# Second step of the rotary turn and the two sums with the attention sink on GpSimd instead of VectorE, in a two-layer hybrid decoder

## The chip, the cores and the metric

The kernel runs on one core of one Trainium2 chip. The metric is the device time of one execution in microseconds (us): the median of several runs of the same program. One execution was also taken by the hardware profiler; what is read from a trace is of that one.

The engines go by the profile's names: PE (TensorE, matrix products and transposes), PEld (its weight loads), DVE (VectorE), ACT (ScalarE), POOL (GpSimd), SP (SyncE, which here issues the transfers). Each works through its own list of instructions in order, and waits where an operand comes from another engine.

## What is computed

Two decoder layers over 512 tokens of width 1024, all in fp32. Each layer projects its input once into the queries, keys and values of two groups of heads and of an indexer, runs the two attentions, projects back, adds and normalises, and ends with a gated feed-forward part. Cut to what the change touches:

```python
def rope(x, positions):                       # x: queries or keys, last axis d = 64 or 32
    cos, sin = jnp.cos(ang), jnp.sin(ang)     # ang = positions * inv_freq, d/2 angles
    x1, x2 = x[..., :half], x[..., half:]
    return jnp.concatenate([x1 * cos - x2 * sin, x2 * cos + x1 * sin], -1)

def swa_sink_attention(q, k, v, sinks):       # group "a": window of 128 keys, 8 heads, 2 key heads
    s = jnp.einsum('bnqhgd,bnkhd->bnhgqk', qb, kb_window) * (D ** -0.5)   # masked
    m = jnp.maximum(s.max(-1, keepdims=True), sink)
    pr = jnp.exp(s - m)
    denom = pr.sum(-1, keepdims=True) + jnp.exp(sink - m)
    return (pr / denom) @ v_window

def dsa_sparse_attention(...):                # group "b": 8 heads, 1 key head
    # indexer: relu(qi . ki) weighted and summed over 8 heads of 32; the 128 best keys of each query
    # attention over these keys, no sink

def hybrid_layer(...):
    qa, ka, va, qb, kb, vb, qi, ki, wi = split(x @ w_in)
    # rope on qa, ka, qb, kb, qi and on layer_norm(ki)
    x = layer_norm(alpha * x + concat(oa, ob) @ w_o)
    x = layer_norm(alpha * x + ffn(x) + ple)
```

## The kernel before

The 512 tokens are four tiles of 128, with the tokens of a tile on the 128 partitions. A product of two fp32 matrices is made of three matmuls in the format fp32r: high times high, high times low and low times high (L316 to L318). So each operand is split: ACT copies it to fp32r (the high part), and POOL or DVE subtracts that from the fp32 original (the low part). For the weights SP fetches a block into one of three buffers `wst`, ACT copies (L269), POOL subtracts (L270) into one of five buffers `wsp`; the down projection does the same at L247 and L248.

A rotary turn (`rope`) has four instructions per call. DVE multiplies the projection's result, still in PSUM, by a table that holds cosine and sine beside each other, into a temporary `t2k` in SBUF (L474). The second step adds the two products, one of them with its halves swapped, within `t2k` (L476). ACT copies the sum to its high part in a `slot` (L479), and POOL makes the low part (L480). Later `turn` or the functions `turns` transpose the slot on PE (L486), and ACT copies the result out of PSUM (L487). Each layer makes 32 such calls: 16 for the queries of the two attentions (256 sums per partition), 8 for the queries of the indexer (128) and, for the keys, 2 + 4 smaller ones (64 or 128).

The indexer multiplies turned queries and keys (PE, L617), ACT applies relu (L619), DVE sums over heads (L620). Its keys are first normalised on DVE (from L526 over L350, L542 and L353 to L360 to L543), then turned. A search on DVE finds the 128 best keys: 16 rounds of L631 and L632 for each of three tiles.

Attention goes by units of four heads and 128 queries. `scores` runs PE (L656) and, for each head, a DVE instruction that adds the mask and keeps the row's minimum (L659). In group a, L664 takes the sink into that minimum. ACT makes the exponentials with their row sums (L666). For the sink, L669 adds sink and minimum (4 values per partition), ACT takes its exponential (L670), and L671 adds that to the row sums. DVE takes the reciprocal (L672), and POOL spreads it over 256 columns (`rb`, L674). `values` transposes the exponentials (L700), copies them (L703, L708), multiplies by the values (L694), transposes `rb` (L717), copies it (ACT, L720), scales (DVE, L725) and splits (L732, L733).

What is issued when is decided twice. A class `Order` interleaves the streams of work by ratios written into the kernel, and puts the transposes off behind the turn by fixed amounts of PE work (`D_GI, D_K, D_Q` of L36, `order.later`). Then the Tile scheduler, with a timeline of its own for the costs, arranges the instructions of each engine, so a change of an instruction's engine also moves others.

Of the kernel before, what the change touches and what calls it, by code (L numbers as in the profile page):

```python
# [14 lines left out]
OP = mybir.AluOpType  # L15
# [72 lines left out]
def hybrid_kernel(ctx: ExitStack, tc: tile.TileContext, x, p, positions, ln_in_g, ln_in_b, w_in,  # L88
# [3 lines left out]
    PE, V, A, G, SP = nc.tensor, nc.vector, nc.scalar, nc.gpsimd, nc.sync  # L92
# [11 lines left out]
    def bank(tag, bufs, dt=F32):  # L104
        return psum.tile([128, 512], dt, name="bank", tag="bank", bufs=8)
# [7 lines left out]
    def t2k(dt=F32):  # L113
        return tmp.tile([128, 512], dt, name="t2k", tag="t2k")

    def sm(n, name):
        return small.tile([128, n], F32, name=name, tag=name)
# [347 lines left out]
    def rope(src, t, n, d, hi, lo, dup, each=False):  # L465

        h = d // 2  # L470
        tab = tab64 if d == 64 else tab32
        tab = tab[:, t:t + n] if each else tab[:, t, None].to_broadcast([128, n, 2, d])
        t12 = t2k()[:, :2 * n * d].rearrange("p (n c d) -> p n c d", n=n, c=2)
        V.tensor_tensor(t12, src[:, :, None].to_broadcast([128, n, 2, d]), tab, OP.mult)  # L474
        t1, t2 = t12[:, :, 0], t12[:, :, 1]
        V.tensor_tensor(t1.rearrange("p n (u i) -> p n u i", u=2), t1.rearrange("p n (u i) -> p n u i", u=2),  # L476
                        t2.rearrange("p n (u i) -> p n u i", u=2)[:, :, ::-1], OP.add)
        s = t1 if dup == 1 else t1[:, :, None, :].to_broadcast([128, n, dup, d])
        A.copy(hi, s)  # L479
        G.tensor_tensor(lo, s, hi, OP.subtract)  # L480
# [30 lines left out]
    for l in range(L):  # L511
# [6 lines left out]
        def gi_out(t, ps):  # L518
# [10 lines left out]
            if t > 0:  # L529
                wi[t] = small.tile([128, IH], F32, name="wi", tag="wi", bufs=4)  # L530
                V.tensor_scalar(wi[t], ps[:, 288:296], IH ** -0.5 * ID ** -0.5, None, op0=OP.mult)
                qs = [slot(), slot()]
                r1 = ps[:, :256].rearrange("p (n d) -> p n d", n=IH)
                for j in range(2):
                    qv = qs[j].rearrange("p (n u s d) -> p n u s d", n=4, u=2, s=2)
                    rope(r1[:, 4 * j:4 * j + 4], t, 4, ID, qv[:, :, :, 0], qv[:, :, :, 1], 2)
# [68 lines left out]
        def wait(*keys):  # L605
            while not all(k in ready for k in keys):
                yield None
# [30 lines left out]
        def scores(kind, t, g, st):  # L638
            if kind == "a":
                k0, nk, c = max(0, t - 1) * 128, (256 if t else 128), g  # L640
                mask = win if t else win[:, 128:]
                yield from wait((kind, t, g), *[("k", b) for b in range(max(2, t + 1))])
            else:
                k0, nk, c = 0, (t + 1) * 128, 2
                yield from wait((kind, t, g), *[("k", b) for b in range(max(2, t + 1))], *[("s", t)] * (t > 0))
                mask = work[t] if t else causal[:, S - 128:]
            nn = max(nk, 256)
            per = 512 // nn
            ng, sums = sm(4, "ng"), sm(4, "sums")
            es = []  # L650
            for j in range(4):
                if j % per == 0:
                    ps, e = bank("sc", 2), t2k()
                o = j % per * nn
                for s in range(2):
                    PE.matmul(ps[:, o:o + nn], qT[kind, t, g][:, j * 128:(j + 1) * 128], kT[c, s][:, k0:k0 + nn],  # L656
                              start=(s == 0), stop=(s == 1))
                es.append(e[:, o:o + nk])
                V.tensor_tensor_reduce(es[j], ps[:, o:o + nk], mask, -HD ** -0.5, 3e38, op0=OP.add, op1=OP.min,  # L659
                                       accum_out=ng[:, j:j + 1])  # L660
                yield 0.44 * nn / 512
            if kind == "a":
                sk = sink[:, l, 4 * g:4 * g + 4]
                V.tensor_tensor(ng, ng, nsink[:, l, 4 * g:4 * g + 4], OP.min)  # L664
            for j in range(4):
                A.activation(es[j], es[j], AF.Exp, bias=ng[:, j:j + 1], scale=-1.0, accum_out=sums[:, j:j + 1])  # L666
            if kind == "a":
                ek = sm(4, "ek")
                V.tensor_tensor(ek, sk, ng, OP.add)  # L669
                A.activation(ek, ek, AF.Exp)  # L670
                V.tensor_tensor(sums, sums, ek, OP.add)  # L671
            V.reciprocal(sums, sums)  # L672
            rb = small.tile([128, 256], F32, name="rb", tag="rb", bufs=3)
            G.tensor_copy(rb.rearrange("p (j d) -> p j d", j=4), sums[:, :, None].to_broadcast([128, 4, 64]))  # L674
            st.extend([es, rb, k0 // 128, nk // 128])
# [260 lines left out]
        for gi, fs in enumerate(GROUPS):  # L936
# [27 lines left out]
            for h in range(2):  # L964
                ps = [acc() for _ in range(NT)]
                n = len(hs)
# [78 lines left out]
```

## Time and profile before

| | |
|---|---|
| time, median of 3 runs (lowest to highest) | 1295.43 us (1294.8 to 1296.61) |
| the profiled execution | 1295.42 us, its span 1293.6 us, so 1.8 us lie around the span |
| PE busy | 1244.4 us, 96% of the span |
| DVE busy | 837.7 us, 65% |
| POOL busy | 666.8 us, 52% |
| ACT busy | 575.7 us, 44% |
| mean granted clock of PE | 0.985 of full speed |

The profiled execution took what the median run took, so sums made on its trace can be set against the median. PE is busy for all but 49 us of the span. An engine's share over the span is a mean over stages that are unlike each other: the input projection and attention of layer 0 lie at about 20 to 230 us, those of layer 1 at about 660 to 860 us, and the rest is output projection and feed-forward part.

### The profile page before, as it was taken

The numbers are of one execution on the slowest core, as the hardware profiler recorded it, in microseconds if no ns is written. First come the engines' busy times: TensorE is split into PE (matmuls) and PEld (weight loads), VectorE is DVE, ScalarE is ACT, GpSimd is POOL, SyncE is SP. The second block draws the span as 40 slices with busy tenths as digits, with TensorE's granted clock in tenths as the row PEclk, the third lists the DMA queues.
The fourth block names the chain that finished last, engine by engine and source line by source line (L and its number), as shares of the span: only waits on it lengthen the run. The fifth ranks groups of instructions, "written<-read, shape, count | busy, mean of one in ns | idle before, by whom it ended". The sixth has DMA issues, their size and how long they took to land.

```text
span 1293.6 us, 18329 instructions
## 1 busy us (share of the span) xinstructions
PE 1244.4 (96%) x6632; PEld 1073.3 (83%) x6632; DVE 837.7 (65%) x1866; ACT 575.7 (44%) x1216; POOL 666.8 (52%) x477
## 2 busy tenths in 40 slices
PE   6799999899999999999998999998999999999996
PEld 4799889788888888888897997888888888888885
DVE  8899965864545453635679997765827273636276
ACT  2656765343343433333337576744434343434220
POOL 7565432357475757563155544414665665757422
PEclk9799999999999999999998999999999999999998
DMA  5133121332232424134032313103342414231321
GB/s 171 50 98 99 58 74 33 98 109 92 94 114 82 129 67 131 33 114 136 2 97 70 111 34 98 50 17 128 101 126 70 139 59 145 67 113 34 114 82 49
DMA packets 89123, 112.77 MB, mean 87 GB/s; under 512 B 5444, under 2 KB 65860, under 8 KB 89032
## 3 DMA queue, kind: packets, MB, share of 16 engines
q1 hardware_dynamic: 88360, 111.58, 27.8%
q8 instruction: 52, 0.85, 0.3%
q14 instruction: 39, 0.32, 0.1%
q10 hardware_dynamic: 672, 0.03, 0.0%
HBM read 109.49 MB, written 2.10 MB: 86 GB/s over the span
## 4 chain that ended last, share of the span: by engine, by line
PE 81%; DVE 12%; ACT 2%; issue 2%; DMA 1%; POOL 1%; DVEq 0%; SPq 0%; POOLq 0%; ACTq 0%
PE bank L316 24%; PE bank L317 24%; PE bank L318 24%; PE bank L656 2%; PE bank L700 2%; DVE t2k L476 2%; PE bank L694 2%; DVE work L620 1%; DVE m L631 1%; DVE work L632 1%; DVE t2k L474 1%; DMA wst<-in_w_pg_dram 1%; DVE x L404 1%; POOL wsp L270 1%; PE bank L486 1%
## 5 line engine op out<-in xcount | busy, mean ns | idle before, releaser
L270 POOL TENSOR_TENSOR wsp<-wst,wsp 128x1024 fp32r<-128x1024 f32 (+2 forms) x148 | 353.4, 2402 | 273.4 <-ACT wsp L269 271.2
L317 PE MATMUL bank<-fl,wsp 128*128 128x512 f32 (+1 forms) x768 | 284.9, 372 | 2.0 <-DVE fl L415 2.0
L316 PE MATMUL bank<-fh,wsp 128*128 128x512 f32 (+1 forms) x768 | 283.6, 372 | 1.0 <-ACT fh L414 1.0
L318 PE MATMUL bank<-fh,wsp 128*128 128x512 f32 (+1 forms) x768 | 283.2, 371 | 0.0
L269 ACT CAST wsp<-wst 128x1024 fp32r<-128x1024 f32 (+2 forms) x148 | 151.3, 1032 | 158.3 <-PE bank L318 108.1
L843 DVE TENSOR_TENSOR t2k<-bank,t2k 128x512 f32<-128x512 f32 x44 | 30.4, 692 | 222.2 <-PE bank L318 222.2
L317 PEld LDWEIGHTS bank<-fl,wsp 128*128 128x128 f32 x768 | 144.7, 188 | 27.4 <-DVE fl L415 2.4
L316 PE MATMUL bank<-wsp,fh 128*128 128x256 f32 (+3 forms) x512 | 165.9, 326 | 0.7 <-ACT fh L414 0.3
L318 PE MATMUL bank<-wsp,fl 128*128 128x256 f32 (+3 forms) x512 | 164.6, 323 | 1.5 <-DVE fl L415 1.5
L316 PEld LDWEIGHTS bank<-fh,wsp 128*128 128x128 f32 x768 | 143.6, 188 | 26.6 <-ACT fh L414 1.9
L318 PEld LDWEIGHTS bank<-fh,wsp 128*128 128x128 f32 x768 | 144.7, 188 | 24.9
L317 PE MATMUL bank<-wsp,fh 128*128 128x256 f32 (+3 forms) x512 | 164.4, 321 | 0.0
L248 POOL TENSOR_TENSOR wsp<-slot,wsp 128x512 fp32r<-128x512 f32 x100 | 141.5, 1439 | 28.5 <-ACT wsp L247 28.5
L316 PE MATMUL bank<-wsp,slot 128*128 128x512 f32 x392 | 153.5, 392 | 0.0
L317 PE MATMUL bank<-wsp,slot 128*128 128x512 f32 x392 | 152.7, 390 | 0.0
L775 DVE TENSOR_TENSOR x<-bank,x 128x512 f32<-128x512 f32 x140 | 91.5, 686 | 88.5 <-PE bank L318 88.5
L318 PE MATMUL bank<-wsp,slot 128*128 128x512 f32 x392 | 148.4, 389 | 0.0
L875 ACT CAST slot<-t2k 128x256 fp32r<-128x256 f32 (+1 forms) x104 | 49.8, 497 | 144.1 <-DVE t2k L843 102.5
L248 POOL TENSOR_TENSOR wsp<-t2k,wsp 128x512 fp32r<-128x512 f32 x40 | 57.5, 1448 | 93.0 <-ACT wsp L247 93.0
L316 PEld LDWEIGHTS bank<-wsp,fh 128*128 128x128 f32 x512 | 98.3, 192 | 7.5 <-ACT fh L414 1.0
L318 PEld LDWEIGHTS bank<-wsp,fl 128*128 128x128 f32 x512 | 97.9, 192 | 7.1 <-DVE fl L415 2.1
L317 PEld LDWEIGHTS bank<-wsp,fh 128*128 128x128 f32 x512 | 98.4, 192 | 5.4
(166 smaller groups left out, 2189.4 us busy)
## 6 DMA issues: line engine op xcount, KB each, us to landing
wst<-in_w_gu_dram SPq DMA_DIRECT2D x88, 512.0 KB, 3.5
slot<-in_w_down_dram SPq DMA_DIRECT2D x80, 256.0 KB, 2.8
wst<-in_w_in_dram SPq DMA_DIRECT2D x16, 512.0 KB, 3.6
wst<-in_w_o_dram SPq DMA_DIRECT2D x16, 512.0 KB, 3.7
wst<-in_w_pg_dram SPq DMA_DIRECT2D x16, 512.0 KB, 4.0
wst<-in_w_in_dram SPq DMA_DIRECT2D x8, 256.0 KB, 2.8
lng<-in_ln_g_dram SPq DMA_DIRECT2D x4, 512.0 KB, 6.3
lnb<-in_ln_b_dram SPq DMA_DIRECT2D x4, 512.0 KB, 6.3
```

Source lines behind the costliest of these rows:

```text
L248: G.tensor_tensor(w[:, 1, j], src[j], w[:, 0, j], OP.subtract)
L269: A.copy(w[:, 0, :a * n], st[:, :a * n])
L270: G.tensor_tensor(w[:, 1, :a * n], st[:, :a * n], w[:, 0, :a * n], OP.subtract)
L316: PE.matmul(o, sh, mh, start=start, stop=False, skip_group_check=again)
L317: PE.matmul(o, sh, ml, start=False, stop=False, skip_group_check=again)
L318: PE.matmul(o, sl, mh, start=False, stop=stop, skip_group_check=again)
L476: V.tensor_tensor(t1.rearrange("p n (u i) -> p n u i", u=2), t1.rearrange("p n (u i) -> p n u i", u=2), t2.rearrange("p n (u i) -> p n u i ...
L656: PE.matmul(ps[:, o:o + nn], qT[kind, t, g][:, j * 128:(j + 1) * 128], kT[c, s][:, k0:k0 + nn], start=(s == 0), stop=(s == 1))
L694: PE.matmul(o, vt[b0 + b][:, f:f + 128], pts[b][:, u], start=b == 0 and u == 0, stop=b == nb - 1 and u == 1)
L775: V.tensor_tensor(xt[t][:, c], ps, xt[t][:, c], OP.add)
L843: V.tensor_tensor(a, ps[1, f], a, OP.mult)
L875: A.copy(h[0], src)
```

## The change

Three instructions get another engine; what they compute, and on what, stays.

```diff
         V.tensor_tensor(t12, src[:, :, None].to_broadcast([128, n, 2, d]), tab, OP.mult)
         t1, t2 = t12[:, :, 0], t12[:, :, 1]
-        V.tensor_tensor(t1.rearrange("p n (u i) -> p n u i", u=2), t1.rearrange("p n (u i) -> p n u i", u=2),
+        G.tensor_tensor(t1.rearrange("p n (u i) -> p n u i", u=2), t1.rearrange("p n (u i) -> p n u i", u=2),
                         t2.rearrange("p n (u i) -> p n u i", u=2)[:, :, ::-1], OP.add)
...
                 ek = sm(4, "ek")
-                V.tensor_tensor(ek, sk, ng, OP.add)
+                G.tensor_tensor(ek, sk, ng, OP.add)
                 A.activation(ek, ek, AF.Exp)
-                V.tensor_tensor(sums, sums, ek, OP.add)
+                G.tensor_tensor(sums, sums, ek, OP.add)
             V.reciprocal(sums, sums)
```

That is L476 (64 instructions in the whole program), L669 (16) and L671 (16). Where they stand on POOL is the scheduler's choice. Three places follow, in rows of the instruction lists: line, operation, output<-inputs with the buffers' numbers, and shape.

The first is POOL's list in the indexer's part of layer 0. Here `wsp` is a weight's low part, `slot` a turned operand's low part, and `t2k` a rotary temporary; 365, 370, 473, 478, 545 and 550 are queries of the indexer, and 398 and 578 its keys, of which 578 are the last. Before:

```order
L270 TENSOR_TENSOR wsp_507<-wst_149,wsp_507 128x768
L270 TENSOR_TENSOR wsp_521<-wst_152,wsp_521 128x768
L480 TENSOR_TENSOR slot_363<-t2k_365,slot_363 128x8x32
L270 TENSOR_TENSOR wsp_532<-wst_155,wsp_532 128x1024
L480 TENSOR_TENSOR slot_364<-t2k_370,slot_364 128x8x32
L480 TENSOR_TENSOR slot_397<-t2k_398,slot_397 128x2x64
L480 TENSOR_TENSOR slot_471<-t2k_473,slot_471 128x8x32
L480 TENSOR_TENSOR slot_472<-t2k_478,slot_472 128x8x32
L480 TENSOR_TENSOR slot_543<-t2k_545,slot_543 128x8x32
L480 TENSOR_TENSOR slot_544<-t2k_550,slot_544 128x8x32
L480 TENSOR_TENSOR slot_577<-t2k_578,slot_577 128x2x64
```

Now, from the fifth row of the same stretch on (the additions of 365 and 370, the split of 507 and the addition of 398 stand ahead of it, in this order):

```order
L476 TENSOR_TENSOR t2k_473<-t2k_473 128x4x32
L480 TENSOR_TENSOR slot_363<-t2k_365,slot_363 128x8x32
L476 TENSOR_TENSOR t2k_478<-t2k_478 128x4x32
L270 TENSOR_TENSOR wsp_521<-wst_152,wsp_521 128x768
L480 TENSOR_TENSOR slot_364<-t2k_370,slot_364 128x8x32
L270 TENSOR_TENSOR wsp_532<-wst_155,wsp_532 128x1024
L480 TENSOR_TENSOR slot_397<-t2k_398,slot_397 128x2x64
L476 TENSOR_TENSOR t2k_545<-t2k_545 128x4x32
L480 TENSOR_TENSOR slot_471<-t2k_473,slot_471 128x8x32
L476 TENSOR_TENSOR t2k_550<-t2k_550 128x4x32
L480 TENSOR_TENSOR slot_472<-t2k_478,slot_472 128x8x32
L476 TENSOR_TENSOR t2k_578<-t2k_578 128x2x32
```

The additions have been slipped in between the weight splits and the low parts; the last of them, for the keys 578, stands ahead of the low parts of 543 and 544.

The second place is POOL's list at the same point of layer 1; 6597 and 6602 are the last queries of the indexer, 6630 its last keys, 6798 keys of the attention. Before:

```order
L270 TENSOR_TENSOR wsp_6559<-wst_6279,wsp_6559 128x768
L270 TENSOR_TENSOR wsp_6573<-wst_6291,wsp_6573 128x768
L270 TENSOR_TENSOR wsp_6584<-wst_6303,wsp_6584 128x1024
L480 TENSOR_TENSOR slot_6595<-t2k_6597,slot_6595 128x8x32
L480 TENSOR_TENSOR slot_6596<-t2k_6602,slot_6596 128x8x32
L480 TENSOR_TENSOR slot_6629<-t2k_6630,slot_6629 128x2x64
```

Now:

```order
L270 TENSOR_TENSOR wsp_6559<-wst_6279,wsp_6559 128x768
L270 TENSOR_TENSOR wsp_6573<-wst_6291,wsp_6573 128x768
L270 TENSOR_TENSOR wsp_6584<-wst_6303,wsp_6584 128x1024
L476 TENSOR_TENSOR t2k_6597<-t2k_6597 128x4x32
L476 TENSOR_TENSOR t2k_6602<-t2k_6602 128x4x32
L476 TENSOR_TENSOR t2k_6630<-t2k_6630 128x2x32
L476 TENSOR_TENSOR t2k_6798<-t2k_6798 128x2x64
L480 TENSOR_TENSOR slot_6595<-t2k_6597,slot_6595 128x8x32
L480 TENSOR_TENSOR slot_6596<-t2k_6602,slot_6596 128x8x32
L480 TENSOR_TENSOR slot_6629<-t2k_6630,slot_6629 128x2x64
```

Four additions now stand behind the three weight splits and ahead of the three low parts.

The third place is POOL's list late in the attention of layer 1; `sums` and `ek` are the row sums and the sink's term of a unit, `rb` its reciprocals, `t2k` with `slot` 7945 and 7951 query turns. Before:

```order
L733 TENSOR_TENSOR slot_7924<-t2k_7889,slot_7924 128x256
L674 COPY rb_7814<-sums_7737 128x256
L270 TENSOR_TENSOR wsp_8041<-wst_7322,wsp_8041 128x1024
L480 TENSOR_TENSOR slot_7945<-t2k_7946,slot_7945 128x4x64
L480 TENSOR_TENSOR slot_7951<-t2k_7952,slot_7951 128x4x64
L270 TENSOR_TENSOR wsp_8151<-wst_7579,wsp_8151 128x1024
L674 COPY rb_7910<-sums_7832 128x256
L733 TENSOR_TENSOR slot_7999<-t2k_7971,slot_7999 128x256
L674 COPY rb_8012<-sums_7928 128x256
```

Now:

```order
L476 TENSOR_TENSOR t2k_7946<-t2k_7946 128x4x64
L733 TENSOR_TENSOR slot_7924<-t2k_7889,slot_7924 128x256
L476 TENSOR_TENSOR t2k_7952<-t2k_7952 128x4x64
L480 TENSOR_TENSOR slot_7945<-t2k_7946,slot_7945 128x4x64
L674 COPY rb_7910<-sums_7832 128x256
L270 TENSOR_TENSOR wsp_8041<-wst_7322,wsp_8041 128x1024
L480 TENSOR_TENSOR slot_7951<-t2k_7952,slot_7951 128x4x64
L733 TENSOR_TENSOR slot_7999<-t2k_7971,slot_7999 128x256
L669 TENSOR_TENSOR ek_8007<-sink_79,ng_7927 128x4
L270 TENSOR_TENSOR wsp_8151<-wst_7579,wsp_8151 128x1024
L671 TENSOR_TENSOR sums_7928<-sums_7928,ek_8007 128x4
L669 TENSOR_TENSOR ek_8091<-sink_79,ng_8014 128x4
```

The copy `rb_7910` has moved ahead of both weight splits, and the sum of unit 7928, for which DVE's reciprocal L672 waits, now has the split 8151 ahead of it.

## Rows read from the trace of the kernel before

**Rows 1.** The page's line of busy time, share of the span, and instructions.

```profile
PE 1244.4 (96%) x6632; PEld 1073.3 (83%) x6632; DVE 837.7 (65%) x1866; ACT 575.7 (44%) x1216; POOL 666.8 (52%) x477
```

**Rows 2.** Stretches: length; busy PE, PEld, DVE, ACT, POOL; PE's clock, DMA share, GB/s.

```profile
40.00:60.00 20.00, 13.96 (x80) 12.84 (x79) 17.52 (x45) 10.41 (x27) 10.35 (x13) 0.75 0.30 80
140.00:160.00 20.00, 18.58 (x141) 17.31 (x139) 19.80 (x69) 16.27 (x53) 9.83 (x10) 1.00 0.27 82
780.00:800.00 20.00, 17.02 (x91) 13.88 (x89) 17.09 (x63) 13.73 (x50) 7.33 (x12) 0.91 0.35 113
```

**Rows 3.** What PE waited for over the span: total us, times, longest.

```profile
PE bank L617 <- ACT slot L487: 11.6, 2, 5.9
PE bank L656 <- DVE ng L659: 2.8, 6, 1.3
PE bank L700 <- ACT t2k L720: 2.1, 1, 2.1
PE bank L700 <- DVE ng L659: 1.3, 1, 1.3
```

**Rows 4.** Groups by line, shapes apart: count | busy us, mean ns | idle before.

```profile
L476 DVE TENSOR_TENSOR t2k<-t2k 128x256 f32<-128x256 f32 x32 | 20.9, 676 | 0.0
L476 DVE TENSOR_TENSOR t2k<-t2k 128x128 f32<-128x128 f32 x20 | 15.2, 780 | 0.0
L476 DVE TENSOR_TENSOR t2k<-t2k 128x64 f32<-128x64 f32 x12 | 4.5, 378 | 0.0
L669 DVE TENSOR_TENSOR ek<-sink,ng 128x4 f32<-128x4 f32 x16 | 4.3, 266 | 0.0
L671 DVE TENSOR_TENSOR sums<-sums,ek 128x4 f32<-128x4 f32 x16 | 4.6, 286 | 0.0
L480 POOL TENSOR_TENSOR slot<-t2k,slot 128x256 fp32r<-128x256 f32 x52 | 38.7, 757 | 62.5 <-ACT slot L479 62.4
L480 POOL TENSOR_TENSOR slot<-t2k,slot 128x128 fp32r<-128x128 f32 x12 | 5.9, 491 | 19.4 <-ACT slot L479 19.4
```

**Rows 5.** The instructions of L476: shortest, median and longest ns.

```profile
L476 DVE TENSOR_TENSOR t2k<-t2k x64: 208/416/2495, 39.0 to 790.0; 128x256 f32<-128x256 f32 x32, 128x128 f32<-128x128 f32 x20, 128x64 f32<-128x64 f32 x12
```

**Rows 6.** Timeline, layer 0, the indexer's start: start us, us, instruction [idle before].

```profile
38.20 3.81 POOL L270 TENSOR_TENSOR wsp<-wst,wsp 128x768 fp32r<-128x768 f32 x2 [1.64 <-ACT wsp L269]
39.01 6.98 DVE L476 TENSOR_TENSOR t2k<-t2k 128x128 f32<-128x128 f32 x5
52.16 0.23 DVE L476 TENSOR_TENSOR t2k<-t2k 128x64 f32<-128x64 f32 x1
53.53 2.73 PE L617 MATMUL bank<-slot 128*128 128x256 f32 x8 [5.75 <-ACT slot L487]
```

**Rows 7.** Timeline, layer 1, the same point.

```profile
672.16 6.05 POOL L270 TENSOR_TENSOR wsp<-wst,wsp 128x768 fp32r<-128x768 f32 x3
675.04 3.31 DVE L476 TENSOR_TENSOR t2k<-t2k 128x128 f32<-128x128 f32 x2
678.88 0.79 DVE L542 SCALAR_TENSOR_TENSOR kin<-kin,kmv,ikg 128x32 f32<-128x32 f32 x1
684.18 2.14 PE L617 MATMUL bank<-slot 128*128 128x256 f32 x7 [5.89 <-ACT slot L487]
```

**Rows 8.** Timeline, three places in the attentions of both layers.

```profile
150.76 2.38 POOL L270 TENSOR_TENSOR wsp<-wst,wsp 128x1024 fp32r<-128x1024 f32 x1 [0.24 <-ACT wsp L269]
151.41 1.75 DVE L669 TENSOR_TENSOR ek<-sink,ng 128x4 f32<-128x4 f32 x1
733.33 2.01 DVE L476 TENSOR_TENSOR t2k<-t2k 128x256 f32<-128x256 f32 x1
778.75 2.37 POOL L270 TENSOR_TENSOR wsp<-wst,wsp 128x1024 fp32r<-128x1024 f32 x1
780.38 0.75 DVE L664 TENSOR_TENSOR ng<-ng,nsink 128x4 f32<-128x4 f32 x1
785.77 0.66 PE L700 MATMUL bank<-idf,t2k 128*128 128x128 f32 x4 [2.09 <-ACT t2k L720]
```

## The prediction

> **What bounds the kernel now.** I read the page's busy times first. PE works 96% of the span and DVE 65% [rows 1], so work taken from DVE is worth only what it brings forward on PE, and all gaps of PE together are 1293.6 - 1244.4 = 49 us. The next view, the stretches, shows where DVE could matter [rows 2]: in the attention of layer 0 (140 to 160 us) it is busy 19.80 of 20 us while PE does 18.58; at 40 to 60 us PE does only 13.96, and at 780 to 800 us 17.02, both at a granted clock under 1. The third, what PE waited for, gives the gaps names [rows 3]: 11.6 us in two waits of the indexer's first matmuls (L617) for ACT's copy, 2.8 us of score matmuls (L656) for DVE's L659, which has to empty a bank, 2.1 us of transposes (L700) for ACT, and 1.3 us of them for L659. Every one of them lies where turns or sink sums are made.
>
> The groups by line and L476's own instructions show what DVE would lose [rows 4, 5]. L476 takes 676 ns for 256 sums and 780 for 128, so the smaller form is the slower, and single ones run from 208 to 2495 ns about a median of 416. Such a spread is waiting, not work. The timeline says for what: five of L476 took 6.98 us while POOL was in weight splits that began at 38.20 us [rows 6]; two took 3.31 us beside POOL's three splits of 6.05 us [rows 7]; and an L669 of four values took 1.75 us, ending with the split that POOL had begun at 150.76 us [rows 8]. Beside POOL such a DVE instruction stands still until POOL's present one ends, and what is behind it in DVE's list stands too.
>
> The Trainium skill has a rule for this: by "SBUF — State Buffer", section "Who interferes with whom", a DVE instruction with both inputs in SBUF and a GpSimd instruction that reads SBUF share a pair of ports, which the first holds for its whole length while the other is fully blocked. The spread of L476 agrees.
>
> **What the change takes and adds.** DVE loses 20.9 + 15.2 + 4.5 us of L476, 4.3 of L669 and 4.6 of L671, together 49.5 us [rows 4]. Of L476's 40.6 us, work is about 32 x 0.42 + 20 x 0.29 + 12 x 0.21 = 22 us (the median for the 256 form, the shortest for the 64 form, between them for 128) [rows 5], and some 19 us are waiting.
>
> POOL gains them. No row shows a POOL addition of these shapes within fp32; the nearest is its subtraction L480, 757 ns for 256 and 491 for 128 [rows 4]. Below, it can hardly be quicker than DVE's unhindered 0.42 and 0.29; above, I allow twice L480. I take L480 itself (same engine, two inputs, same shapes). The line through its two forms is 0.225 us and 2.08 ns per value: 0.36 us for 64, 0.23 for 4. So POOL gains 32 x 0.757 + 20 x 0.491 + 12 x 0.36 + 32 x 0.23 = 46 us (30 to 90 by the bounds). It goes from 667 to about 713 us, 55%, still with room in every stage of [rows 2], the fullest of which has it at 10.35 of 20.
>
> What counts is the path at PE's gaps.
>
> *Layer 0, the wait of 5.75 us before 53.53.* It hangs on the last keys of the indexer: L476 at 52.16, done at 52.39, then ACT's copy, transposes and a copy to L617 [rows 6]. Before it DVE lost its 6.98 us, less some 5 x 0.29. In the new list POOL comes from 38.20 to that addition over two splits (3.81), one of 1024 columns (2.38, [rows 8]), four L480 of 128x256 (3.03), one of 128 (0.49), the addition of 398 (0.36) and four of 128 sums (1.96): 12.0 us, so at 50.2, and ends at 50.6; the additions of 365 and 370 fit into the 1.64 us in which POOL stood idle ahead of 38.20. DVE, rid of its waiting, has the product by then. Gain 52.4 - 50.6 = 1.8 us, and I take 1.7. Bounds: POOL additions of DVE's length take 1.1 us less in all and give 2.9; of twice L480, 2.7 more and -0.9.
>
> *Layer 1, 5.89 us before 684.18* [rows 7]. POOL's splits end at 672.16 + 6.05 = 678.2 either way. DVE now starts to normalise the keys at 675.04 instead of 678.3, but with instructions that also read SBUF; L542 ended at 678.88 + 0.79 = 679.67. If they wait for the splits once more, L542 ends at about 678.4: gain 1.3. If they slip through, all 3.3 us are gained. Two L476 waited in just this place, so I take 1.9, nearer the lower end.
>
> *Attention* [rows 8]. With L669 gone from 151.41 the L659 behind it comes 1.6 us sooner, which closes the 1.34 us of [rows 3]: gain 1.3. The L476 at 733.33 took 2.01 instead of 0.42, again 1.6 us, against a wait of 1.33 of L656: gain 1.3. At 785.77 L700 waited 2.09 us for ACT, whose exponentials had waited for L664 at 780.38, and that for DVE's queue; several moved instructions and their waits lie just ahead of it, and the new list puts `rb_7910` before the splits. Gain 2.1, bounds 0 and 2.1.
>
> Sum: 1.7 + 1.9 + 1.3 + 1.3 + 2.1 = 8.3 us.
>
> *What is given back.* L672 on DVE now waits for POOL's L671, and in the new list a split of 2.37 us [rows 8] can stand between L669 and L671, as for unit 7928. Behind L672 in DVE's list are L659s and the search, and behind those PE's score banks. Bounds: nothing, where the split ran before ACT's exponentials were done anyway; 2.4 us on PE in each of 16 units at the worst. I take two places that lose 2.4 us of DVE, half of it reaching PE, which is 2.4 us. Turns become 0.34 us longer each (0.757 - 0.416) and sometimes queue behind a split; their transposes are put off by a fixed amount of PE work, so this costs nothing while that cover lasts. In the indexer's start it doesn't, and is counted above.
>
> Net -5.9: from the profiled execution's 1295.4 us (equal to the median shown) to 1289.5 us.
>
> The Trainium skill speaks against the change: "GPSIMD Engine Reference", section 4.1 "Engine selection", keeps elementwise additions on VectorE, GpSimd being about twice as slow with two inputs. The rows agree on the price, 757 ns beside a median of 416, 1.8 times. By that rule alone 22 us of work become 46, and the change loses; by the rows it trades a slower instruction on an engine at 52% for waiting on one that has no time left.
>
> **Rivals.** *POOL becomes what is waited for* (slower). L671 and L476 stand in one list with 2.4 us splits, and ACT, which used to wait for DVE, waits for POOL with exponentials behind it. Against it: L476 on DVE already waited for the same splits. If six of the 16 sink units put a whole split on PE's path, it costs 6 x 2.4 = 14.3, less the 8.3: about 1301 us. It decides from four units on (8.3 / 2.4 = 3.5). Chance 0.17. The skill's rule on elementwise work would show itself in this way.
>
> *It is hidden.* PE is the bound at 96%, and what DVE gives free goes into the search, which nobody waits for; in the indexer's gaps POOL's longer list (twice L480) takes what DVE won. Then 1294 to 1296 us. For it: over most of the span DVE isn't missed. Against it: the gaps of [rows 3] have DVE's stalled instructions right ahead. Chance 0.14.
>
> *More is won*: the gaps get short enough for the clock to stay up. At 40 to 60 us PE ran 13.96 us at 0.75, which at full clock is 10.5, so 3.5 us less; the same in layer 1; at 780 to 800, 17.02 x 0.09 = 1.5. Together 8.5 more: 1281 us. Against it: by the sum above, over 3.5 us of each indexer gap remain. Chance 0.11.
>
> **The numbers.** The likeliest case, 1289.5 us, has 0.58, and by itself spans 1286 to 1293 (the bounds of the two indexer gaps and of the L672 wait). A measurement of this kernel can tell about 0.2%, 2.6 us, from no change, so faster is below 1292.8 and slower above 1298.0. Faster: nearly all of the likeliest case (0.55) and the clock case, 0.66. Same: the hidden case and the rest of the likeliest, 0.17. Slower: 0.17. The range for 8 in 10 leaves about 1 in 10 at each end: 1283 to 1298.5.
>
> **What would show each step.** Right: DVE's busy time 45 to 50 us lower, POOL's 40 to 50 higher, with L476 on POOL near 0.75, 0.49 and 0.36 us; L617 of layer 0 about 1.7 us earlier and of layer 1 about 1.9, still with gaps of 3.5 to 4.5 us and a low clock behind; no wait of L700 or L656 for L659 above 0.5 us; DVE idle before L672, up to 2.4 us in a few units. Wrong: idle time of DVE before L672 in many units, with PE's L656 or L717 waiting behind it; L476 on POOL beyond 1 us; or DVE's other two-input instructions, L659 aside, growing by what L476 lost.

## The result

The changed kernel takes 1288.17 us in the median of 4 runs (1286.75 to 1290.64), beside 1295.73 us for the kernel before (1294.8 to 1296.61). The ratio is 0.9944, with a 95% interval of 0.9927 to 0.9961: 7.3 us less, which is more than the 0.2% (2.6 us) that the prediction took a measurement to tell. The forecast was 1289.5. The profiled execution took 1287.86 us with a span of 1286.1.

The page's busy line of the changed kernel, to be set beside [rows 1]:

```profile
PE 1244.0 (97%) x6632; PEld 1074.7 (84%) x6632; DVE 810.7 (63%) x1770; ACT 573.9 (45%) x1216; POOL 706.2 (55%) x573
```

PE does the same work; DVE is busy 27.0 us less and POOL 39.4 us more. The groups by line, shapes apart, show both sides (count, then busy us and mean ns, then idle before); the first five answer to [rows 4]:

```profile
L476 POOL TENSOR_TENSOR t2k<-t2k 128x256 f32<-128x256 f32 x32 | 23.6, 748 | 6.8 <-DVE t2k L474 6.6
L476 POOL TENSOR_TENSOR t2k<-t2k 128x128 f32<-128x128 f32 x20 | 10.1, 514 | 10.8 <-DVE t2k L474 10.7
L476 POOL TENSOR_TENSOR t2k<-t2k 128x64 f32<-128x64 f32 x12 | 3.9, 323 | 8.7 <-DVE t2k L474 8.7
L671 POOL TENSOR_TENSOR sums<-sums,ek 128x4 f32<-128x4 f32 x16 | 3.2, 201 | 11.3 <-ACT ek L670 11.0
L669 POOL TENSOR_TENSOR ek<-sink,ng 128x4 f32<-128x4 f32 x16 | 3.2, 200 | 11.9 <-DVE ng L664 10.6 <-DVE sums L672 1.1
L634 DVE TENSOR_SCALAR work<-work 128x256 f32<-128x256 f32 x2 | 4.6, 2280 | 0.0
L664 DVE TENSOR_TENSOR ng<-ng,nsink 128x4 f32<-128x4 f32 x16 | 5.4, 338 | 0.0
L542 DVE SCALAR_TENSOR_TENSOR kin<-kin,kmv,ikg 128x32 f32<-128x32 f32 x8 | 5.1, 641 | 0.0
L353 DVE TENSOR_SCALAR lns<-lnv 128x2 int32<-128x2 int32 x4 | 3.2, 808 | 0.0
```

On POOL the additions cost what L480 let one expect: 748, 514, 323 and 200 ns (taken: 757, 491, 360 and 230), together 44.0 us. On DVE 49.5 us went, but its busy time fell by 27.0 only. The last four rows show where a part came back: in the trace of before, this form of L634 (the last step of the search) took 528 ns on the mean, L664 273, L542 409 and L353 156. These four lines together have 9.2 us more than before. Instructions behind the moved ones now meet POOL's splits themselves. L634 and L353 have a single SBUF operand, so two are not needed to wait.

What PE waited for over the span (total us, times, longest), beside [rows 3]:

```profile
PE bank L617 <- ACT slot L487: 7.5, 2, 5.0
PE bank L694 <- ACT t2k L708: 1.9, 3, 1.1
PE bank L656 <- DVE ng L659: 1.3, 3, 0.6
PE bank L486 <- POOL slot L480: 0.9, 1, 0.9
```

And the stretches of [rows 2]:

```profile
40.00:60.00 20.00, 16.15 (x88) 14.56 (x86) 13.54 (x41) 11.81 (x33) 14.62 (x21) 0.83 0.29 80
140.00:160.00 20.00, 18.26 (x129) 16.44 (x129) 13.87 (x53) 16.67 (x55) 15.16 (x23) 1.00 0.31 94
```

Both waits of L700 are gone and that of L617 is 4.1 us shorter, but L694 now waits for ACT, and L486 for POOL. At 140 to 160 us DVE fell from 19.80 to 13.87 and PE gained nothing (18.26 after 18.58).

Shares of busy time don't tell where the 7.5 us of span went, so I compared PE's instructions one by one. Both traces hold the same number of matmuls, 6632, and at more than nine tenths of the places in the sequence the same one. The start of the k-th in one minus that of the k-th in the other, both counted from the first, says how far ahead one kernel is there; the difference between two such points is what a stage gained (-) or lost (+). In us, the stages by the times of the kernel before; the columns are the change and nine of the experiments below:

```
stage (us of before)    change  e1    e2    e3    e12   e4    e6    e10   e7    e11
start, to 41             +0.7  +0.0  +0.2  +0.9  +0.2  +0.1 +10.1  +0.3  +2.5  +1.7
indexer 0, 41-77         -2.6  -4.3  +0.1  -3.2  -0.2  -1.7  -1.4  -0.0  -6.2  -3.7
attention 0, 77-171      -0.9  +0.2  -0.0  +3.0  -0.8  +4.1  +4.0  +2.5  -0.7  +0.0
171-662                  +0.7  -0.2  +0.0  -0.2  +0.5  +1.8  -0.1  +0.5  +1.3  +0.0
indexer 1, 662-702       +0.1  +0.0  +0.0  -0.2  +0.6  +0.1  +0.0  +0.3  -3.3  -0.6
attention 1a, 702-740    -1.7  -1.7  -1.2  +2.0  -1.7  -1.7  -1.3  -0.8  -1.7  -1.7
attention 1b, 740-779    -0.3  -1.1  +0.2  -0.8  -0.3  +0.2  +0.2  +0.3  -0.3  -0.3
attention 1c, 779-801    -3.8  -1.6  -4.1  -0.1  -3.8  -2.6  -2.7  -2.8  -3.8  -3.8
801-1276                 +0.2  +2.0  +0.8  -0.1  -0.0  +2.8  +0.1  +1.7  +1.8  +0.9
sum                      -7.5  -6.7  -3.9  +1.3  -5.6  +2.9  +8.8  +2.1 -10.4  -7.5
```

It is of one execution each, and most kernels' runs differ by 2 to 4 us, so a sum can stand off its median (the traces of e1 and e12 are of their fastest runs, 1288.72 with a median of 1292.1 and 1289.86 with one of 1292.44).

### The profile page after: what moved, and what is told of

Its sections match the earlier page's. It is cut to its first block, busy times and chain, and to the rows that moved or that the text cites. A ratio compares the mean times of both kernels' runs of the same rounds, so it can differ in the third digit from the quotient of the medians.

```text
span 1286.1 us, 18307 instructions
## 1 busy us (share of the span) xinstructions
PE 1244.0 (97%) x6632; PEld 1074.7 (84%) x6632; DVE 810.7 (63%) x1770; ACT 573.9 (45%) x1216; POOL 706.2 (55%) x573
## 4 chain that ended last, share of the span: by engine, by line
PE 85%; DVE 7%; ACT 3%; issue 2%; POOL 2%; DMA 1%; DVEq 0%; SPq 0%; POOLq 0%; ACTq 0%
PE bank L316 26%; PE bank L317 26%; PE bank L318 25%; PE bank L656 2%; PE bank L700 2%; PE bank L694 2%; POOL wsp L270 1%; DVE work L620 1%; PE bank L412 1%; PE bank L486 1%; DVE x L404 1%; DMA wst<-in_w_pg_dram 1%; ACT t2k L666 1%; PE bank L717 0%; ACT wsp L269 0%
```

## The experiments

Medians are of 4 to 12 runs; a ratio is to runs of the kernel before on the same chip, whose median there was 1296.8 to 1297.7 us.

**One part at a time.** e1 moves L476 alone:

```diff
-        V.tensor_tensor(t1.rearrange("p n (u i) -> p n u i", u=2), ...
+        G.tensor_tensor(t1.rearrange("p n (u i) -> p n u i", u=2), ...
```

> Only the addition of the rotary turn (L476) is on GpSimd; the two sink sums stay on VectorE. Theory W (waits): what counted is that L476 stood still on VectorE beside GpSimd's weight splits, right ahead of the gaps of TensorE. Then this part alone brings the gain at the indexer's start of layer 0 (about 1.9 us) and of the L476 that waited at 733 us (1.3 to 1.9 us), and some of the 3.8 us at 780 to 800 us: 1289 to 1291 us, L476's own share being two thirds or more. Theory S (sink sums): the gain came from the shorter way between L664, the sums and the reciprocal; then this one stays within 2 us of before, 1294 to 1296 us.

Measured: 1292.1 us, ratio 0.9956 (0.9943 to 0.9969), so 5.7 us less, beside 7.3 of the whole change; the stages are the indexer of layer 0 and attention 1a, as theory W had it, and 1c only in part. The -4.3 of the indexer is not L476's alone: 1.6 us of it are the clock's, as the section on the low clock shows.

e2 moves the two sums alone (L669 and L671 from `V` to `G`).

> Only the two sums with the sink (L669, L671) are on GpSimd; L476 stays on VectorE. Theory W: gain only where an L669 waited beside a split (about 1.3 us at 151 us) and part of the 3.8 us at 780 to 800 us: 1292 to 1295 us. Theory S: most of the gain, 1288 to 1291 us. If the reciprocal's wait for GpSimd costs more than the sums give, it is slower than before, 1296 to 1298 us.

Measured: 1292.24 us, ratio 0.9961 (0.9949 to 0.9974), so 5.1 us less. The time lies in W's range, but against the 1297.15 us of before on this chip the gain is more than W's 0.7 to 3.7, and all of it is in layer 1: nothing in the indexer, nothing in layer 0's attention, 4.1 us in 1c. So the place at 151 us that I had put down to L669 gave nothing, and 1c gave twice what was thought. The two parts alone, 5.7 and 5.1 us, are more than the 7.3 of both together.

e3 moves L476 only where d is 32, that is for the indexer.

```diff
-        V.tensor_tensor(t1.rearrange(
+        (G if d == 32 else V).tensor_tensor(t1.rearrange(
```

> L476 is on GpSimd for the turns of the indexer's queries and keys only (d = 32); those of the attentions and the sink sums stay on VectorE. Theory W: the indexer's start of layer 0 gains 1.5 to 2 us, that of layer 1 nearly nothing, as in the change's trace, the attentions nothing: 1293 to 1294.5 us. If the indexer's start were worth in both layers what was forecast (1.7 and 1.9 us): 1291.5 to 1292.5 us.

Measured: 1296.7 us, ratio 1.0001 (0.9992 to 1.001). The indexer of layer 0 came out as expected (+0.9 and -3.2), layer 1's gave nothing, but the attentions, in which no instruction has another engine, lost 3.0 and 2.0 us. This is not a new arrangement: by line, tile and shape PE, DVE and ACT have the same order as before from 77 to 171 us, and nearly the same from 702 to 740. What changed is when the instructions of L476 left on DVE meet a split. The first row is of before, the others are of e3, which comes to this point 2.3 us ahead:

```profile
85.62 0.21 DVE L476 TENSOR_TENSOR t2k<-t2k 128x64 f32<-128x64 f32 x1
```

```profile
85.30 2.39 POOL L270 TENSOR_TENSOR wsp<-wst,wsp 128x1024 fp32r<-128x1024 f32 x1 [1.34 <-ACT wsp L269]
85.42 2.34 DVE L476 TENSOR_TENSOR t2k<-t2k 128x64 f32<-128x64 f32 x1
88.15 0.28 PE L583 MATMUL bank<-idr,slot 128*128 128x128 f32 x1 [0.94 <-ACT slot L479]
107.52 0.50 PE L656 MATMUL bank<-slot 128*128 128x256 f32 x2 [1.29 <-DVE ng L659]
```

The last wait lies behind an L476 that took 1.77 us at 105.48; before, it took 1.92 at 104.64 and PE waited for nothing there. So L476 beside a split took away again what L476 off it had won. The 2.0 us at 734 to 740 are treated with the prediction's steps. e12 is the complement, `G if d == 64 else V` with the sums on POOL:

> The change without its indexer part: L476 on GpSimd only for the turns of the attentions (d = 64), with both sink sums; the indexer's turns keep L476 on VectorE. Theory A (places add up): layer 0's indexer start gains nothing, the place at 733 us 1.3 to 1.9 us, the end of layer 1's attention 3 to 4 us as in the change: 1290 to 1292 us, against 1288 with the indexer. Theory R (rearranged): what a place gives depends on how the scheduler happens to arrange everything behind the first moved instruction, as the indexer's part alone gave 2.3 us in layer 0 and lost them again in the attentions; then the end of layer 1's attention comes out anywhere between nothing and 4 us, the median between 1289 and 1297 us, and the two parts do not add up to the change.

Measured: 1292.44 us, ratio 0.9962 (0.9948 to 0.9976). Its column is that of the change, to 0.5 us, in every stage but the start and layer 0's indexer, where it has nothing: -5.6 in all, as the change has without these two. So the indexer's -1.9 is kept where the attentions' L476 have left DVE, and was lost in e3, where they had not.

**Waiting or work?** In e4 everything stays on DVE, but L476 takes its second operand from the projection's bank in PSUM, so it isn't a rotary turn any more:

```diff
-                        t2.rearrange("p n (u i) -> p n u i", u=2)[:, :, ::-1], OP.add)
+                        src.rearrange("p n (u i) -> p n u i", u=2)[:, :, ::-1], OP.add)
```

> L476 and the sink sums stay on VectorE, but L476 takes its second operand from the projection's bank in PSUM instead of from the product with the sine (so the turn is not the rotary turn; same shape, same count). It has one operand in SBUF now. Theory W: its waits beside the weight splits vanish, VectorE's L476 falls from 40 us to 22 to 24 us in all with no instruction over 0.6 us, and the time falls to 1289 to 1292 us though VectorE keeps all its instructions. Rival (VectorE is simply full, and each of its us counts): only about half of L476's part comes back, 1293 to 1294 us. If the second step was not waiting for ports at all, the long ones stay, and so does the time, 1295 to 1297 us.

Measured: 1299.29 us, ratio 1.0013 (1.0004 to 1.0022). Its L476 by shortest, median and longest ns, for the 60 that read PSUM (the four of the indexer's keys take both operands from SBUF as before, and the longest of them took 230):

```profile
L476 DVE TENSOR_TENSOR t2k<-t2k,bank x60: 200/402/417, 38.0 to 790.2; 128x256 f32<-128x256 f32 x32, 128x128 f32<-128x128 f32 x20, 128x64 f32<-128x64 f32 x8
```

That settles the first half: with one operand out of SBUF the longest is 417 ns, where [rows 5] had 2495, so the other time was waiting beside POOL. The Trainium skill, "SBUF — State Buffer", section "Who interferes with whom", says that a DVE instruction with at most one SBUF input contends with GpSimd only in its two-port modes; the trace agrees. The time nevertheless did not fall. Up to 152 us e4 was ahead by 3.1 us, the change by 2.6. Then, at the end of layer 0's attention, it lost 5.5 us. Rows of the timeline there, with waits in brackets:

```profile
148.36 2.37 POOL L270 TENSOR_TENSOR wsp<-wst,wsp 128x1024 fp32r<-128x1024 f32 x1
149.12 1.63 DVE L664 TENSOR_TENSOR ng<-ng,nsink 128x4 f32<-128x4 f32 x1
151.91 0.42 PE L700 MATMUL bank<-idf,t2k 128*128 128x128 f32 x2 [1.99 <-DVE ng L659]
156.73 2.08 PE L694 MATMUL bank<-t2k,slot 128*128 128x256 f32 x4 [1.44 <-ACT t2k L708]
```

And the stretch behind the first wait (length; busy PE, PEld, DVE, ACT, POOL; clock, DMA share, GB/s):

```profile
152.00:160.00 8.00, 6.38 (x23) 4.97 (x24) 7.91 (x30) 7.70 (x29) 2.10 (x4) 0.51 0.27 97
```

With L476 out of the way it was L664, another instruction with two SBUF operands, that stood beside the split: 1.63 us, where its median before was 0.15. PE's two waits came close together behind it, and the clock stood at its lower level (1.2 GHz is 0.5) for these 8 us. So taking the waits of L476 away brings the gains of layer 0's start and of 1a, and does not by itself make the kernel faster: the wait can pass to another instruction.

**What the indexer's gaps hang on.** After the change 2.6 and 5.0 us of them were left. e5 is the change, e6 the kernel before, both with the indexer's transposes put off by 8 instead of 9 us:

```diff
-D_GI, D_K, D_Q, AHEAD = 9.0, 8.0, 10.0, 2
+D_GI, D_K, D_Q, AHEAD = 8.0, 8.0, 10.0, 2
```

> The changed kernel with the indexer's transposes put off by 8 instead of 9 us of TensorE work (D_GI). ScalarE's copies of finished transposes (L487), for which the first L617 waits, then stand ahead of the copies of the last turns (L479) in ScalarE's list instead of behind them. Theory O (order): the gap at the indexer's start that the change left open, 2.6 and 5.0 us, hangs on this place in the list and not on how fast the addition L476 is made; the gaps shrink to 1 us or less, the clock stays up or comes back sooner, and the time falls by 4 to 12 us against the changed kernel, to 1277 to 1285 us. Theory P (path): the gap hangs on the keys' own way through normalising, addition and copy; then the copies wait elsewhere and the time stays within 2 us of the changed kernel's.

> The kernel before with the same delay of 8 instead of 9, everything else on VectorE as before. Theory O: the indexer's gaps of 5.8 and 5.9 us shrink here too, by 2 us or more each, and the time falls to 1285 to 1292 us; the difference between this kernel and the one with the change and a delay of 8 is then the attention's part alone, 4 to 6 us. Theory P: 1294 to 1298 us, no change.

Measured: e5 1295.27 us, ratio 0.9989 (0.9979 to 0.9998); e6 1302.34 us, ratio 1.0046 (1.003 to 1.0061). Both theories missed a cost. The transposes had moved ahead of the low parts that they read, and POOL makes those behind its weight splits: PE's longest wait, of L486 for L480, was 9.5 us (7.6 in e6). As a test of the order of ACT's list it is inconclusive, but it shows how thin the cover of the turns is.

e7 is the change with the keys normalised tile by tile, as soon as they are there. The first step reads PSUM, so neither the copy L525 nor a second SBUF operand is needed:

```diff
-            A.copy(kin[t - u][:, u], ps[:, 256:288])
             V.bn_stats(st, ps[:, 256:288])
             V.bn_aggr(kmv[t - u][:, u], st)
+            V.scalar_tensor_tensor(kin[t - u][:, u], ps[:, 256:288], kmv[t - u][:, u, 0:1], ikg[:, l], ...
+            rs = rstd_of(kmv[t - u][:, u, 1:2])
+            V.scalar_tensor_tensor(kin[t - u][:, u], kin[t - u][:, u], rs, ikb[:, l], ...
...
-                rs = rstd_of(mv[:, :, 1], 2)
-                for i in range(2):
...
```

> The changed kernel with the indexer's keys normalised tile by tile as soon as they are there, the first step reading them from PSUM (no copy L525, no second SBUF operand in L542). The results are the same. In the change's trace L350 and L542 of layer 1 stood 1.3 and 2.5 us beside the weight splits. Theory P: without these waits and with half of the chain the keys are turned 2 to 3 us sooner in layer 1 and 1 us in layer 0, and the time falls by 3 to 6 us against the changed kernel. Theory O: the copies L487 still stand behind L479 in ScalarE's list, but that one is done sooner, so the two theories differ little here; if the keys get done sooner and the time does not move, something else holds ScalarE's list.

Measured: 1284.74 us, ratio 0.9912 (0.9899 to 0.9924): about 3.5 us better than the change, and faster than both kernels. Against the kernel before, layer 1's indexer gains 3.3 us (the change: nothing) and layer 0's 3.7 with its start counted (the change: 1.9). PE's waits there are 4.6 us in all, after 7.5. So the gaps did hang on the keys' own chain. What in the chain it was is not separated. In layer 1 the way from the first step on the last keys (L526, here L525) to their product L474 is 6.2 us instead of 8.2; the copy that was waited for is gone, there are fewer steps, and the waiting beside the splits is less but not gone, for the second step of the normalisation still takes both operands from SBUF:

```profile
673.36 2.18 DVE L530 SCALAR_TENSOR_TENSOR kin<-kin,lns,ikb 128x32 f32<-128x32 f32 x1
```

e8 has both edits:

> Both: keys tile by tile, and a delay of 8. Theory O: not more than 1 to 2 us better than the delay of 8 alone, since the keys are no longer waited for. Theory P: better than either alone by the sum, 1279 to 1283 us.

Measured: 1285.77 us, ratio 0.9916 (0.9904 to 0.9929), not different from e7. Neither theory's number came: with the keys done sooner, e5's wait of 9.5 us is gone, and the shorter delay brings nothing more.

**What the low clock costs there.** e9 (on e7), e10 (on the kernel before) and e11 (on the change) put 24, 48, and 24 and 40 transposes of the identity into PE's list right ahead of the first L617; nobody reads them.

```diff
+                if t == 1:
+                    pd = bank("tp", 2, F32R)
+                    for i in range(24):
+                        PE.transpose(pd[:, i % 4 * 128:(i % 4 + 1) * 128], idr, idr)
                 ready.add(("i", t))
```

> The kernel with the keys normalised tile by tile, and 24 transposes of the identity, whose results nobody reads, in TensorE's list right ahead of the first L617 of each layer, where it stood idle for 2.6 and 2.0 us. They add nothing to what is computed. Theory C (clock): a good part of what a gap costs is the low clock behind it, which in that kernel's trace was 0.57 for 8 us in layer 0; with TensorE at work in the gap the clock stays at full and the time falls by 3 to 6 us, to 1279 to 1282 us. Theory G (gap alone): the idle time is all that a gap costs; then the time stays, or rises by up to 1 us where the transposes outlast the gap.

> The kernel before with 48 such transposes in each of the two gaps of 5.8 and 5.9 us. Theory C: the low clock behind them (0.50 to 0.63 for some 16 us in layer 0, 0.50 to 0.55 for 8 us in layer 1) goes, and the time falls by 6 to 10 us, to 1286 to 1291 us, as much as the change brought. Theory G: 1295 to 1299 us.

> The changed kernel with 24 such transposes in the gap of layer 0 and 40 in that of layer 1. Theory C: 1280 to 1285 us, 4 to 8 us below the changed kernel. Theory G: 1287 to 1291 us.

Measured: e9 1285.04 us, ratio 0.9909 (0.9895 to 0.9923); e10 1295.97, ratio 0.9999 (0.9989 to 1.0009); e11 1287.14, ratio 0.9934 (0.9914 to 0.9954). All three stay where their base was. But only e9 has a gap behind which the clock stayed at full for 8 us, that of layer 0. In e10 and e11 PE still waited 1.1 to 2.2 us for ACT in each gap, and the clock fell behind them: e10 had 0.50 at 56 to 60 us and at 691 to 695, e11 0.75 and, at 683 to 687, 0.50. Layer 0 in stretches of 8 and 4 us, first of e7:

```profile
52.00:60.00 8.00, 7.69 (x33) 5.93 (x33) 6.25 (x17) 7.45 (x23) 2.70 (x7) 0.57 0.12 43
60.00:64.00 4.00, 3.00 (x15) 2.75 (x16) 4.00 (x16) 2.99 (x12) 3.08 (x8) 1.00 0.01 2
```

Then of e9:

```profile
52.00:60.00 8.00, 5.14 (x32) 3.59 (x30) 6.75 (x18) 7.62 (x25) 3.29 (x9) 1.00 0.06 20
60.00:64.00 4.00, 3.50 (x11) 3.25 (x12) 4.00 (x14) 2.16 (x10) 2.59 (x7) 0.66 0.01 2
```

And one of PE's waits in e9, where L620 and L623 are the lines L617 and L620 of the kernel before:

```profile
PE bank L620 <- DVE work L623: 3.5, 6, 1.3
```

For 8 us the clock did stay at full, and PE did nearly the same work in 5.14 us instead of 7.69; but it then waited, for DVE's sums over heads with ACT full beside it. e9 is 0.46 us ahead of e7 at the first matmul of the indexer and 0.45 ahead at the last one of this stretch: the low clock had cost nothing there, because another engine set the pace. Then e9's clock fell after all (0.66 at 60 to 64 us), with PE at work on the next projection, and nine matmuls of 0.52 us, which take 0.33 to 0.35 in e7, are most of what put it 1.1 us behind e7.

Among the traces kept there is one in which the clock came back sooner behind the same gap. e1 has PE's instructions in the change's order up to here and the same wait of 2.6 us. The change:

```profile
64.00:68.00 4.00, 4.00 (x20) 3.96 (x19) 3.93 (x13) 0.00 (x0) 0.23 (x1) 0.76 0.00 0
```

And e1:

```profile
64.00:68.00 4.00, 4.00 (x24) 3.88 (x23) 3.90 (x13) 2.44 (x4) 0.78 (x1) 1.00 0.00 0
```

PE is full in both. Ten matmuls of the projection that took 0.53 us in the change took 0.33 in e1, which gained 1.6 us on the change there. So at this gap the low clock was free while PE waited for DVE anyway, and cost about 1.5 us where PE was full.

## Why the prediction was right, step by step

The sum came out 1.3 us from the measured time, and this closeness is in part luck. Two terms worth 3.2 us (layer 1's indexer, the L669 at 151 us) gave nothing, the 2.4 us given back did not come either, and the end of layer 1's attention gave 1.7 us more than forecast.

*Layer 0's indexer: right.* Forecast -1.7, measured -1.9 (start and indexer together); e3 alone has -2.3 there and e12 +0.0, so it is shown to be the indexer's L476. The timeline of the changed kernel, beside [rows 6]:

```profile
48.63 0.48 DVE L474 TENSOR_TENSOR t2k<-kin,tab 128x128 f32<-128x128 f32 x1
50.76 0.73 POOL L476 TENSOR_TENSOR t2k<-t2k 128x64 f32<-128x64 f32 x2
52.22 2.69 PE L617 MATMUL bank<-slot 128*128 128x256 f32 x8 [2.56 <-ACT slot L487]
```

DVE had its product at 49.1 and POOL came to the addition at 50.8 (forecast 50.2): POOL's list is what is waited for now, as forecast.

*Layer 1's indexer: the step that failed.* Forecast -1.9, measured +0.1. I had two ends, 1.3 if L350 and L542 waited for the splits once more, 3.3 if not. They waited (beside [rows 7]):

```profile
670.73 5.99 POOL L270 TENSOR_TENSOR wsp<-wst,wsp 128x768 fp32r<-128x768 f32 x3
673.04 1.35 DVE L350 TENSOR_SCALAR lnv<-kmv 128x2 f32<-128x2 f32 x1
674.31 2.46 DVE L542 SCALAR_TENSOR_TENSOR kin<-kin,kmv,ikg 128x32 f32<-128x32 f32 x1
681.72 2.73 PE L617 MATMUL bank<-slot 128*128 128x256 f32 x8 [4.99 <-ACT slot L487]
```

The stall of 3.3 us left L476 and came back on the next two instructions as 3.8. L542 now ends with the splits and no longer 1.5 us behind them, as the lower end had it; L353 and L355 behind it then took 0.5 us more than before. Two further prices had been put at nothing. The prediction took POOL's splits to end at the same time either way, but additions now stand ahead of them in POOL's list, and the splits came 0.6 us later than PE's lead of 2.1 us had them; a matmul of the projection waited for one:

```profile
672.63 0.44 PE L317 MATMUL bank<-wsp,fh 128*128 128x384 f32 x1 [0.30 <-POOL wsp L270]
```

PE's gap is 0.9 us shorter, but by 0.6 of that PE came to it later, so L617 starts only 0.3 us further ahead. And 0.6 us were lost at 690 us, where the clock stayed low for longer than before and matmuls took 0.52 us instead of 0.33. e7, in which the keys are done 2 us sooner, has the gain that was missing.

*The L669 at 151 us: the gap closed, the gain didn't come.* Forecast -1.3. The wait of 1.34 us is gone, and four others stand in its place, of 0.18, 0.64, 0.67 and 0.24 us. The longest two:

```profile
153.77 0.50 PE L656 MATMUL bank<-slot 128*128 128x256 f32 x2 [0.64 <-DVE ng L659]
154.95 1.13 PE L694 MATMUL bank<-t2k,slot 128*128 128x256 f32 x4 [0.67 <-ACT t2k L708]
```

That is the hidden case in one place. The -0.9 of this attention comes from another, at 118 to 126 us, which I had not counted.

*The L476 at 733 us: right, a little small.* Forecast -1.3, measured -1.7 in 1a, and -1.7 in e1, e12 and e4 as well. But kernels that leave it on DVE as it was end this stage between 2.0 us behind (e3) and 1.3 ahead (e6). The stall is there in both, 2.00 us at 734.43 in e3 and 1.88 at 745.01 in e6, but PE's wait behind it is 1.61 in the one and 0.18 in the other: its price depends on where PE is when it comes. And in e3 most of the price is the clock's. Its wait is only 0.3 us longer than the 1.33 of before; but in the stretch behind it the clock is 0.60, where before has 1.00 and PE does 33 matmuls:

```profile
736.69 0.74 PE L656 MATMUL bank<-slot 128*128 128x256 f32 x2 [1.61 <-DVE ng L659]
736.00:740.00 4.00, 3.31 (x15) 3.32 (x16) 4.00 (x18) 2.29 (x5) 1.60 (x3) 0.60 0.81 253
```

*The end of layer 1's attention: right in kind, too small, and not all the change's.* Forecast -2.1, measured -3.8. Stretches of 4 us, first of the kernel before:

```profile
776.00:780.00 4.00, 3.77 (x26) 3.27 (x24) 4.00 (x12) 2.36 (x5) 4.00 (x4) 1.00 0.30 89
780.00:784.00 4.00, 2.84 (x20) 1.93 (x18) 4.00 (x17) 2.77 (x12) 2.15 (x3) 1.00 0.47 155
784.00:788.00 4.00, 2.18 (x10) 1.65 (x11) 3.96 (x14) 4.00 (x15) 0.72 (x2) 0.89 0.27 84
788.00:792.00 4.00, 4.00 (x21) 3.47 (x20) 4.00 (x15) 2.80 (x10) 1.59 (x4) 0.68 0.20 66
```

And of the changed kernel, which is 3.9 us ahead as it enters here:

```profile
776.00:780.00 4.00, 3.93 (x30) 3.46 (x30) 3.93 (x15) 4.00 (x15) 2.68 (x4) 1.00 0.19 27
780.00:784.00 4.00, 3.85 (x27) 3.29 (x25) 3.34 (x17) 4.00 (x19) 2.91 (x6) 1.00 0.70 243
784.00:788.00 4.00, 2.94 (x16) 2.51 (x16) 1.12 (x8) 4.00 (x17) 2.77 (x5) 1.00 0.54 169
788.00:792.00 4.00, 4.00 (x24) 3.35 (x22) 0.42 (x1) 0.55 (x3) 0.80 (x2) 1.00 0.20 62
```

PE stood 0.23 + 1.16 + 1.82 = 3.2 us, now 0.07 + 0.15 + 1.06 = 1.3: 1.9 us, about the term forecast. Most of the other 1.9 goes with the clock, at 0.89 and 0.68 before: 2.18 us of work at the one and 4.00 at the other are some 1.5 us more than at full. PE is full in the second of these stretches. I had put such a gain under the rival that more is won, at 1.5 us. But e6 and e10, in which no instruction changes its engine, gain 2.7 and 2.8 us in the same stage. In both, the clock stays at 1.00 there. e3, whose order is nearly that of before, has the low clock (0.81 and 0.76) and gains nothing. So 2.8 of the 3.8 us can come with a new order alone, without any instruction on another engine, and no more than some 1.1 us is left that only the engines can have brought. Which of the two made it in the change is open: the sums alone (e2) have all of it, and the scheduler moved the order with them.

*What is given back: too dear.* Forecast +2.4. The reciprocal L672 of the changed kernel waited for POOL's sum in two places, as taken, but little, and PE waits nowhere for the `rb` behind it. Its view by line, idle time before it in us and how often:

```profile
  POOL sums L671: 1.6, 2
```

The +0.7 of the stretch 171 to 662 us is another thing: the waits at a normalisation near 241 us are the same in both kernels, but the clock fell behind them this time.

*The rivals.* POOL becoming the limit did not happen in the change, though e5 shows it one step away. That the low clock of the indexer's gaps is worth 3.5 us each was not seen: for 8 us behind layer 0's gap e9 shows it to be worth nothing, and behind the same gap e1 shows 1.6 us where PE is full. e10 and e11, where the clock fell all the same, can't tell, and behind layer 1's gap the clock fell in every run. And the Trainium skill's rule against the change ("GPSIMD Engine Reference", section 4.1 "Engine selection"), GpSimd being about twice as slow with two inputs, had the price right and not the outcome. The price here is 748 ns against a median of 416 on DVE.

## What to carry to other kernels

Before crediting an engine with the removal of a stalled instruction, look at the next ones in its list: if they can wait for the same thing, the stall stays and only its owner changes. Move the operand (here into PSUM) rather than the instruction where that ends the waiting, but read the time from the whole kernel. A stall's price depends on where the other engines are when it comes, so a gain in one stage can be lost to the same kind of stall in the next with the order unchanged (e3); and a scheduler rearranges much behind an edit, so that two kernels in which no instruction had changed its engine gained nearly 3 us in one stage. And price a low clock by who sets the pace behind the gap: over 8 us in which PE waited for DVE anyway, full clock brought nothing, and ten matmuls at the lower level with PE full cost 1.6 us.

## What had not been expected of the hardware

A DVE instruction with one SBUF operand waited beside POOL's splits too, down to two values. In layer 0 of the changed kernel, while POOL was in a split (43.25 to 45.10 us):

```profile
43.26 1.87 DVE L353 TENSOR_SCALAR lns<-lnv 128x2 int32<-128x2 int32 x1
```

In e7 the same line works on one value, and beside splits that ran from 43.76 to 49.77 us it did not wait:

```profile
46.30 0.14 DVE L353 TENSOR_SCALAR lns<-lnv 128x1 int32<-128x1 int32 x1
```

The Trainium skill, "VectorE: DVE Perf Modes", section "Mode 2×_2P — use both read ports for one tensor", lets an operation with one source, in SBUF like its result, take both read ports where the outermost dimension longer than one is even. Two values are such a case, and one value has no such dimension; these two rows agree with it.

And the clock's answer to a gap is not settled by the gap alone. At one normalisation of layer 1 PE's waits are the same in the kernel before (1.71, 0.24 and 1.00 us) and in e7 (1.70, 0.24 and 1.00). The stretch with the last two, in the kernel before:

```profile
876.00:880.00 4.00, 2.76 (x21) 2.32 (x20) 4.00 (x12) 3.42 (x7) 4.00 (x3) 1.00 0.61 200
```

And in e7:

```profile
864.00:868.00 4.00, 2.77 (x14) 2.32 (x13) 4.00 (x9) 3.33 (x7) 4.00 (x3) 0.62 0.55 178
```

Only e7's clock fell, which there cost it 1.9 us.
